# A decoder layer on one core: three small carry tiles padded, so that all pools that TensorE reads start at the same address modulo 64 bytes

## The chip, the cores and the metric

The kernel runs on 1 core of one Trainium2 chip. The metric is the device time of one execution in microseconds (us), as the median of several runs. The engines go by their short names in the profile: PE is TensorE's matmul, PEld its load of the stationary operand, DVE is VectorE, ACT is ScalarE, POOL is GpSimd and SP is SyncE, which issues the transfers (DMAs).

## What is computed

One layer of a decoder over 1024 tokens of width 1024, in float32. The reference, cut to its outline:

```python
h = _rms_norm(x, norm_pre_mix)
mix = _hybrid_mixer(h, ...)        # RWKV-7 time mixing of 8 heads beside a causal
                                   # convolution of width 31; one projection in, one out
x = x + _rms_norm(mix, norm_post_mix)
h = _rms_norm(x, norm_pre_ffn)
hid = _causal_dwconv(h @ ffn_up, ffn_conv_w, ffn_conv_b)     # 1024 -> 2 * 2816, width 3
gate, up = hid[..., :2816], hid[..., 2816:]
f = (gelu(gate) * up) @ ffn_down                             # 2816 -> 1024
x = x + _rms_norm(f, norm_post_ffn)
```

Both convolutions reach back over earlier tokens, so whatever works through the tokens in two halves must carry the last columns of the first half over to the second.

## The kernel before

**Precision.** Every large matmul is split: each float32 operand becomes a high part (rounded to float32r by ACT) and a low part (the rest, by DVE or POOL), and a product is three matmuls: high by high, high by low, low by high. `split` (L159) and `weight` (L164) do that. A weight tile is loaded into `wr`, and its halves `wh` and `wl` lie in the pool `wp`.

**Tokens and stages.** The tokens go in two halves of 512. `mixer` (L1245) interleaves the projections, the convolution, the recurrence and the output projection `w_out`, and, near its end, the first twelve tiles of the feed-forward's first half. Then `run` (L1201) opens the feed-forward pools with `setup_ffn` (L817) and goes on in this order:

- `ffn_pair` (L901) of the first half and `gates` (L939): matmuls of the activations `h0`, which lie in the pool `hp`, with weights in `wp`. Beside them the second half is normed; its activations `h1` (named `f` in the profile, as those of `h0` are) go to the pool `h1p`.
- `ffn_pair` of the second half for 12 of the 22 tiles, 48 matmuls each (two branches, 24 each), with `h1` in `h1p` and weights in `wp`. Beside it, `weight_sums` and `four_sums` (L1054) make sums of weight blocks on POOL.
- `shared` (L1004) for the other 10 tiles of both halves: five block products instead of six, 60 matmuls a tile. Its operands are S[2] (pool `rowp`), S[1] (`nrowp`), S[3] and S[4] (written back over `h0` in `hp`), and A22 (`h1[4:]` in `h1p`), all with weights in `wp`.
- `ffn_down` (L1103): seven block products instead of eight, each over 11 tiles of the inner dimension with 12 matmuls. The activations are split into pairs `a` in the pool `h1p`. The weights of the tiles 0, 2, 4, ... lie in `wp` (`wh`, `wl`), those of the tiles 1, 3, 5, ... in `h1p` (`w`), by this line:

```python
wh, wl = self.weight(wt(j), [P, 512], held=self.h1p if j % 2 else None) if j < n else held[j - n]
```

  In the last product the last five tiles' weights lie in `hp` (`held`). In `ffn_down` the activation is the stationary operand and the weight the moving one; in the other stages it is the other way round.

Each matmul instruction comes as a load of the stationary operand (128 columns) and the matmul proper, which streams the moving operand (mostly 512 columns). The load for the next matmul runs beside the matmul before it.

**Order.** The instructions are put in order when the program is built, by a planner with a timeline of its own; each engine then works through its queue in that order and waits on semaphores. Waits and buffers follow from the tiles that an instruction names.

**Memory.** Each pool is a stretch of on-chip memory with the same addresses in all 128 partitions. Pools are laid one behind the other in the order in which they are opened; each tile in a pool is rounded up to a multiple of 32 bytes a partition. `setup` opens `const` (at 16512), `small`, `wp` (at 24192), `hp` (38528) and `rowp` (71296 to 87680). `setup_mixer` opens `mconst` at 87680 and behind it `mix`, at 102752, which holds most of the mixer's tiles. When the mixer is done, the feed-forward takes the same stretch again: `fconst` at 87680, then `nrowp` at 92192, `actp` at 108576, `h1p` at 149536, `tp` at 182304 and `f2p` at 198688.

The three tiles of the change are small. `ccarry` in `mconst` keeps the last 30 columns of the convolution's input for four groups of channels; it is written and read by POOL in `glu_in` (L403, L394). `fcarry` in `fconst` keeps the last two columns of the feed-forward's tiles, written and read by ACT in `taps` (L892, L896). `fss` in `fconst` holds the sums of squares of the last norm: one column of it is written by each ACTIVATE of line L1150 and read by DVE at L1097.

Of the kernel before, what the change touches and what calls it, by code (L numbers as in the profile page):

```python
# [13 lines left out]
F32 = mybir.dt.float32  # L14
# [8 lines left out]
P = 128  # L23
# [13 lines left out]
CONV_W = 31  # L37
D_FF = 2816
FT = D_FF // P
# [59 lines left out]
class Trunk:  # L99
# [116 lines left out]
    def setup_mixer(self, ctx):  # L216
        nc, tc, a = self.nc, self.tc, self.a
        pool = lambda name, bufs=1: ctx.enter_context(tc.tile_pool(name=name, bufs=bufs))
        cp = pool("mconst")
        self.mix = pool("mix")  # L220
        self.banks = {"pb": 2, "pc": 1, "pe": 2}
        self.xs = [self.psum.tile([P, 512], F32, name=f"xs{g}") for g in range(2)]
        self.wa = cp.tile([P, HALF], F32, name="wa")

        self.dw = cp.tile([P, 16 + 1024], F32, name="dw")
        nc.gpsimd.memset(self.dw[0:64, 528:1040], 0.0)
        self.Y = self.psum.tile([P, 512], F32, name="Y")


        self.lora = cp.tile([G_LORA, D_RWKV], F32, name="lora")
        nc.sync.dma_start(self.lora, a["lora"][:G_LORA, 2])
        self.lw = cp.tile([96, 2, D_RWKV], F32R, name="lw")
        for e in range(2):
            raw = self.wp.tile([P, D_RWKV], F32, tag="wr", bufs=3, name=self.nm("wr"))
            nc.sync.dma_start(raw, a["lora"][:, e])
            nc.scalar.copy(self.lw[:, e], raw[0:96])
            low = self.lw[64:96, e]
            nc.gpsimd.tensor_tensor(low, raw[64:96], low.bitcast(F32), ALU.subtract)  # L240
        self.lx = cp.tile([96, 2, QUARTER], F32R, name="lx")
        n = POFF["k_k"]
        self.omu = cp.tile([P, n], F32, name="omu")
        nc.vector.tensor_scalar(self.omu, self.params[:, :n], -1.0, 1.0, ALU.mult, ALU.add)

        self.hw0 = cp.tile([P, 8], F32, name="hw0")
        nc.vector.tensor_scalar(self.hw0, self.params[:, POFF["w0"]:POFF["w0"] + 8], 0.5, None, ALU.mult)
        self.ka = cp.tile([P, 8], F32, name="ka")
        ka = self.params[:, POFF["k_a"]:POFF["k_a"] + 4]
        nc.vector.tensor_scalar(self.ka[:, 0:4], ka, 0.5, None, ALU.mult)  # L250
        nc.vector.tensor_scalar(self.ka[:, 4:8], ka, -0.5, 1.0, ALU.mult, ALU.add)
        cw = self.params[:, POFF["cw"]:POFF["cw"] + 4 * CONV_W]
        nc.vector.tensor_scalar(cw, cw, 0.5, None, ALU.mult)
        self.carry = cp.tile([P, n], F32, name="carry")
        self.ccarry = cp.tile([P, 4, CONV_W - 1], F32, name="ccarry")


    def channels(self, rows, gname, hs, toks, tags=("pn",), diags=None):
# [558 lines left out]
    def setup_ffn(self, ctx):  # L817
        nc, tc = self.nc, self.tc
        pool = lambda name, bufs=1: ctx.enter_context(tc.tile_pool(name=name, bufs=bufs))
        cp = pool("fconst")  # L820

        self.turn = cycle([lambda: self.xs[0], lambda: self.xs[1]]
                          + [lambda t=t: Trunk.bank(self, t) for t in ("pe", "pe", "pb", "pb")])
        self.bank = lambda tag="pb": self.Y if tag == "pn2" else Trunk.bank(self, "pc") if tag == "pn" else next(self.turn)()
        self.nrowp = pool("nrowp")

        self.ap = pool("actp", 2 * JOINT)
        self.h1p = pool("h1p", 2 * KT)
        self.tp = pool("tp", 8)
        self.f2p = pool("f2p", 6)  # L830
        self.post_ffn = cp.tile([P, D], F32, name="post_ffn")
        nc.sync.dma_start(self.post_ffn, self.a["post_ffn"].broadcast_to([P, D]))
        self.fcarry = cp.tile([P, 2, FT, 2], F32, name="fcarry")
        self.fss = cp.tile([P, 8, 2], F32, name="fss")

    def row(self, tag, n):
        return (self.rowp if tag == "row" else self.nrowp).tile([P, D], F32, tag=tag, bufs=n, name=self.nm(tag))
# [630 lines left out]
```

## Time and profile before

| | |
|---|---|
| median of three runs | 1280.13 us (1280.02 to 1281.09) |
| profiled execution | 1282.25 us, of which the span from first to last instruction is 1280.5 |
| mean granted TensorE clock | 0.988 |
| PE busy | 1231.8 us (96%), 8460 matmuls |
| POOL busy | 495.6 us (39%) |

How to read what is quoted further on: the page gives busy time and share of each engine; the 40 digits are the busy tenths of 40 equal slices of the span; the chain is the work that ended last, followed back from the last instruction. A line of the chain in order of time has its start, its length, the engine and line, and the number of instructions merged (x). A window line has for each engine its busy time and the number of instructions, then the granted clock, the busy share of the DMA engines and GB/s. A line of the timeline has the start, the length, the engine, the source line, the operation, the tiles (out<-in, with numbers left out) and sizes, and in brackets the idle time before it and what ended it. Matmuls overlap: one lasts about 0.39 us from its start to its end, while the next starts some 0.23 us after it. The time that matters for a row of matmuls is from start to start.

### The profile page before, as it was taken

The page shows a single profiled execution, that of the slowest core. Times are in us where ns is not written, and L with a number is a line of the kernel's source. Part 1 is how long each engine was busy: PE and PEld are TensorE (multiplying, and loading weights), DVE is VectorE, ACT ScalarE, POOL GpSimd, SP SyncE. Part 2 cuts the span into 40 slices and gives each one's busy share as a digit, 9 for nine tenths or more (in the row PEclk, how much of TensorE's full clock was granted, in tenths as well). Part 3 has the DMA queues.
Part 4 walks back from the last instruction along what each step waited for, and adds up shares of the span by engine and source line. Part 5 has one row for each costly group of instructions (what it writes and reads, how often), then busy time and mean ns, then how long its engine had stood idle before and what let it go on. Part 6 is the DMA issues. An engine that isn't in the chain of part 4 may idle for free.

```text
span 1280.5 us, 23025 instructions
## 1 busy us (share of the span) xinstructions
PE 1231.8 (96%) x8460; PEld 993.7 (78%) x8460; DVE 892.2 (70%) x1540; ACT 731.3 (57%) x1518; POOL 495.6 (39%) x438
## 2 busy tenths in 40 slices
PE   6989989999999989999999999999999999999997
PEld 5767767787778867788789878787778888888885
DVE  5286998997679989996621275655366678479568
ACT  6563564655844865656743277777455566444451
POOL 4343320011113332344455269897688860000001
PEclk9999999999999999999999999999999999999999
DMA  7544442343342461222345498887423245335523
GB/s 241 171 137 138 118 127 76 107 133 116 109 131 89 133 192 44 84 79 80 108 137 159 133 335 304 287 310 238 157 67 82 71 159 190 91 114 187 162 73 132
DMA packets 105505, 185.70 MB, mean 145 GB/s; under 512 B 15184, under 2 KB 21712, under 8 KB 105392
## 3 DMA queue, kind: packets, MB, share of 16 engines
q1 hardware_dynamic: 105392, 184.23, 45.5%
q8 instruction: 67, 1.10, 0.4%
q14 instruction: 46, 0.38, 0.1%
HBM read 141.58 MB, written 42.60 MB: 144 GB/s over the span
## 4 chain that ended last, share of the span: by engine, by line
PE 58%; DVE 8%; issue 2%; POOL 2%; DMA 2%; ACT 2%; SPq 0%; POOLq 0%; DVEq 0%; ACTq 0%
PE pb L135 27%; PE pe L135 13%; PE xs L135 12%; PE Y L135 2%; PE pc L135 2%; DVE pc L416 2%; DVE nrow L1116 1%; POOL wl L162 1%; DVE x L1100 1%; PE pc L150 1%; DMA pt<-mixd 1%; DMA m<-mixd 1%; POOL b L1056 1%; PE pe L150 0%; DVE m L162 0%
## 5 line engine op out<-in xcount | busy, mean ns | idle before, releaser
L162 POOL TENSOR_TENSOR wl<-wr,wh 128x512 fp32r<-128x512 f32 (+1 forms) x181 | 237.5, 1314 | 251.0 <-ACT wh L162 219.8
L162 ACT CAST wh<-wr 128x512 fp32r<-128x512 f32 (+1 forms) x220 | 135.4, 616 | 174.4 <-issue 46.1
L135 PE MATMUL pb<-h,wh 128*128 128x512 f32 (+3 forms) x720 | 228.8, 397 | 3.2 <-ACT wh L162 1.6
L135 PE MATMUL pb<-f,wh 128*128 128x512 f32 x696 | 221.9, 399 | 2.5 <-ACT wh L162 1.5
L416 DVE SCALAR_TENSOR_TENSOR pc<-c,params,pc 128x512 f32<-128x512 f32 x232 | 174.3, 751 | 8.7 <-ACT pc L413 4.7
L135 PEld LDWEIGHTS pb<-h,wh 128*128 128x128 f32 (+2 forms) x720 | 131.2, 188 | 36.0 <-ACT wh L162 3.7
L135 PEld LDWEIGHTS pb<-f,wh 128*128 128x128 f32 x696 | 130.9, 190 | 32.4 <-ACT wh L162 2.8
L135 PE MATMUL pb<-h,wl 128*128 128x512 f32 (+3 forms) x360 | 146.1, 406 | 2.1 <-POOL wl L162 2.0
L135 PE MATMUL pb<-f,wl 128*128 128x512 f32 x348 | 139.0, 400 | 0.9 <-POOL wl L162 0.9
L157 POOL TENSOR_TENSOR ss<-var,mhalf 128x1 f32<-128x1 f32 x16 | 11.0, 692 | 226.9 <-DVE ss L1097 202.8
L1056 POOL TENSOR_TENSOR b<-b,b 128x512 f32<-128x512 f32 x66 | 86.9, 1319 | 2.6 <-DMA b<-ffn_down 1.0
L135 PE MATMUL pe<-f,wh 128*128 128x512 f32 x272 | 85.4, 395 | 0.1
L135 PEld LDWEIGHTS pb<-h,wl 128*128 128x128 f32 (+2 forms) x360 | 67.3, 187 | 20.1 <-POOL wl L162 4.1
L135 PEld LDWEIGHTS pb<-f,wl 128*128 128x128 f32 x348 | 66.3, 190 | 16.7 <-POOL wl L162 2.0
L135 PE MATMUL xs<-f,wh 128*128 128x512 f32 x200 | 62.7, 395 | 0.4 <-DVE act L953 0.4
L135 PEld LDWEIGHTS pe<-f,wh 128*128 128x128 f32 x272 | 51.0, 188 | 11.7 <-ACT wh L162 0.3
L899 DVE SCALAR_TENSOR_TENSOR pt<-pb,params,pt 128x511 f32<-128x511 f32 (+1 forms) x48 | 35.7, 744 | 31.6 <-ACT ecarry L892 31.1
L162 POOL TENSOR_TENSOR wl<-b,wh 128x512 fp32r<-128x512 f32 x36 | 47.0, 1305 | 22.4 <-ACT wh L162 20.7
L135 PE MATMUL pe<-f,wl 128*128 128x512 f32 x136 | 53.8, 396 | 0.7 <-POOL wl L162 0.7
L706 POOL TENSOR_TENSOR XG<-r,GE 64x256 f32<-64x256 f32 x30 | 20.4, 683 | 87.1 <-DVE r L725 82.3
L178 ACT CAST wh<-wr 128x512 fp32r<-128x512 f32 (+2 forms) x44 | 26.5, 604 | 43.5 <-PE pb L135 31.2
L162 ACT CAST wh<-b 128x512 fp32r<-128x512 f32 x36 | 22.2, 617 | 47.4 <-PE pb L135 19.2
(428 smaller groups left out, 2896.8 us busy)
## 6 DMA issues: line engine op xcount, KB each, us to landing
wr<-ffn_up SPq DMA_DIRECT2D x117, 256.0 KB, 2.8
wr<-w_in SPq DMA_DIRECT2D x80, 256.0 KB, 3.0
b<-ffn_down SPq DMA_DIRECT2D x44, 256.0 KB, 4.4
sums<-b SPq DMA_DIRECT2D x44, 256.0 KB, 3.9
wr<-sums SPq DMA_DIRECT2D x44, 256.0 KB, 2.7
lows<-wl SPq DMA_DIRECT2D x40, 256.0 KB, 3.3
wl<-lows SPq DMA_DIRECT2D x40, 256.0 KB, 2.6
b<-ffn_up SPq DMA_DIRECT2D x40, 256.0 KB, 2.7
```

Of the source, the lines that this page charges most:

```text
L135: return self.nc.tensor.matmul(out, lhsT, rhs, start=start, stop=stop, skip_group_check=skip)
L150: self.nc.tensor.transpose(out, in_, self.con("ident")[:n, :n])
L157: self.nc.gpsimd.tensor_tensor(out, v[:, :n], self.mhalf[:, :n], ALU.pow)
L162: return self.nc.scalar.copy(hi, src), eng.tensor_tensor(lo, src, hi.bitcast(F32), ALU.subtract)
L178: self.nc.scalar.copy(hi, raw)
L416: nc.vector.scalar_tensor_tensor(out, c[:, j:j + HALF], w(j), acc, ALU.mult, ALU.add)
L706: nc.gpsimd.tensor_tensor(x[64:128], R[64:128, gs], w.GE[64:128, c, gs].unsqueeze(2).broadcast_to([64, 4, CH]), ALU.mult)
L899: nc.vector.scalar_tensor_tensor(acc[:, o:], ps[:, :HALF - o], w(j), acc[:, o:], ALU.mult, ALU.add)
L1056: sub = lambda o, x, y, op=ALU.subtract: self.nc.gpsimd.tensor_tensor(o, x, y, op)
L1100: nc.vector.scalar_tensor_tensor(x, f[c], s[:, 1:2], x, ALU.mult, ALU.add)
L1116: nc.vector.tensor_tensor(out, a, b, op)
```

## The change

Three tiles are allocated larger than what is used of them. `ccarry` gets 32 columns of which 30 are used, through a view; `fcarry` gets 32 rows instead of 22 in its third dimension; `fss` gets 48 columns, of which the first two are used. In bytes of a partition: 480 to 512, 352 to 512, 64 to 1536. No instruction is added or taken away.

```diff
-        self.ccarry = cp.tile([P, 4, CONV_W - 1], F32, name="ccarry")
+        self.ccarry = cp.tile([P, 4, 32], F32, name="ccarry")[:, :, :CONV_W - 1]
...
-        self.fcarry = cp.tile([P, 2, FT, 2], F32, name="fcarry")
-        self.fss = cp.tile([P, 8, 2], F32, name="fss")
+        self.fcarry = cp.tile([P, 2, 32, 2], F32, name="fcarry")
+        self.fss = cp.tile([P, 8, 48], F32, name="fss")
```

All pools that are opened after these tiles move: `mix` by 32 bytes, and `nrowp`, `actp`, `h1p`, `tp` and `f2p` by 1632. The pools `const`, `wp`, `hp` and `rowp` stay where they are.

## The prediction

> **What bounds the kernel now.** I read the page's first two parts, then the chain, then stretches by engine, then single instructions in order of time.
>
> ```profile
> span 1280.5 us, 23025 instructions
> PE 1231.8 (96%) x8460; PEld 993.7 (78%) x8460; DVE 892.2 (70%) x1540; ACT 731.3 (57%) x1518; POOL 495.6 (39%) x438
> ...
> PE   6989989999999989999999999999999999999997
> ...
> PEclk9999999999999999999999999999999999999999
> ...
> PE 58%; DVE 8%; issue 2%; POOL 2%; DMA 2%; ACT 2%; SPq 0%; POOLq 0%; DVEq 0%; ACTq 0%
> ```
>
> TensorE is busy in nine tenths of nearly every slice at full granted clock, and it holds 58% of the chain. But busy matmuls overlap, so the page cannot say whether the matmuls themselves could go faster. The windows of the feed-forward stages show where nothing else stands in the way:
>
> ```profile
> 780.00:850.00 70.00, 69.58 (x296) 55.09 (x296) 41.19 (x62) 51.33 (x108) 62.83 (x51) 1.00 0.86 297
> 850.00:925.00 75.00, 74.84 (x321) 60.02 (x320) 36.69 (x53) 46.18 (x97) 53.40 (x43) 1.00 0.68 229
> 925.00:1060.00 135.00, 133.61 (x573) 106.33 (x572) 89.59 (x129) 76.56 (x160) 104.10 (x80) 1.00 0.32 100
> 1060.00:1160.00 100.00, 100.00 (x432) 80.91 (x431) 71.03 (x114) 51.61 (x98) 0.00 (x0) 1.00 0.42 135
> ```
>
> The columns are PE, PEld, DVE, ACT, POOL, clock, DMA share, GB/s. PE has no idle worth naming from 780 to 1160, and its clock is 1.00. So the time here is the number of matmuls times the time from one start to the next, and this step is what the change can touch. Is the step the same everywhere? In the chain, pieces of PE follow each other without a gap, so their length over their count is the step:
>
> ```profile
> 762.95 0.44 PE pc L150 x4
> ...
> 772.90 5.47 PE pe L135 x24
> ...
> 841.64 11.24 PE pe L135 x48
> ...
> 864.11 11.25 PE pe L135 x48
> ```
>
> At 773 a 128x512 matmul takes 5.47/24 = 227.9 ns; at 842 and 864 it takes 11.24/48 = 234.2 ns. Same shape, same clock, same instruction line, no waits. What differs is where the operands lie: at 773 the activations come from `hp` (first half of the tokens), at 842 from `h1p` (second half); the weights come from `wp` both times.
>
> **The addresses.** This is the allocator's arithmetic for the kernel before: pools lie one behind the other and each tile is rounded up to 32 bytes a partition. `wp` starts at 24192, `hp` at 38528, `rowp` at 71296: all multiples of 64. `rowp` ends at 87680 = 1370·64. In the mixer the constants up to `ccarry` (rounded: 14400 + 64 + 32 + 32 + 64 + 480 = 15072) put `mix` at 102752 = 1605·64 + 32. In the feed-forward part `post_ffn`, `fcarry` and `fss` (4096 + 352 + 64) put `nrowp` at 92192 = 1440·64 + 32, and `actp`, `h1p`, `tp`, `f2p` behind it keep that 32, since all their tiles are multiples of 64. So a matmul from `hp` with `wp` has both operands in one class modulo 64, one from `h1p` with `wp` has them in two. The change makes `ccarry` 512, `fcarry` 512 and `fss` 1536 bytes: `mix` starts at 102784 = 1606·64, `nrowp` at 93824 = 1466·64. Two classes become one.
>
> Function `shared` gives a control inside one stage, with one weight pool; its order (S[3] and S[4] from `hp`, A22 from `h1p`, then of the next tile S[2] from `rowp`, S[1] from `nrowp`, twelve matmuls each) names each group. The starts:
>
> ```profile
> 950.85 0.62 PE L135 MATMUL pe<-f,wh 128*128 128x512 f32 x2
> ...
> 953.60 0.62 PE L135 MATMUL xs<-f,wh 128*128 128x512 f32 x2
> ...
> 956.32 0.63 PE L135 MATMUL pe<-f,wh 128*128 128x512 f32 x2
> ...
> 959.12 0.63 PE L135 MATMUL pe<-s,wh 128*128 128x512 f32 x2
> ...
> 961.94 0.63 PE L135 MATMUL pb<-s,wh 128*128 128x512 f32 x2
> ...
> 964.75 0.62 PE L135 MATMUL pb<-f,wh 128*128 128x512 f32 x2
> ```
>
> S[3]: 2.75 us over 12 is 229.2 ns; S[4]: 2.72, or 226.7; A22 (two classes): 2.80, or 233.3; S[1] (two classes): 2.81, or 234.2. S[2] (one class) has 2.82, but with a hole in it: its second start waits for a weight. In the last stage, `ffn_down`, both activations `a` and every second weight lie in `h1p`, the other weights (`wh`) in `wp`:
>
> ```profile
> 1148.66 0.62 PE L135 MATMUL pb<-wh,a 128*128 128x512 f32 x2
> ...
> 1151.46 1.55 PE L135 MATMUL pb<-w,a 128*128 128x512 f32 x6
> ...
> 1154.22 0.63 PE L135 MATMUL pb<-wh,a 128*128 128x512 f32 x2
> ...
> 1157.04 1.55 PE L135 MATMUL pb<-w,a 128*128 128x512 f32 x6
> ...
> 1159.80 0.63 PE L135 MATMUL pb<-wh,a 128*128 128x512 f32 x2
> ```
>
> `wh` groups (two classes): 2.80 and 2.82 us. `w` groups (both in `h1p`): 2.76 and 2.76, or 230.0 ns. So it is not `h1p` itself that is slow but the pairing; and a group of one class that follows one of two classes does not get down to 226.7.
>
> **The terms.** No instruction is added or removed; only addresses move.
>
> (1) Pairs of two classes. `ffn_pair` of the second half: 12 tiles x 48 = 576. `shared`: 10 x 12 for A22 and 10 x 12 for S[1] = 240. `ffn_down`: six products with 72 each, and in the last product 36 and the 60 of the held weights: 528. Together 1344. The last product's 96 are left out, for the end is not PE's there:
>
> ```profile
> 1238.47 0.69 DVE L162 TENSOR_TENSOR w<-wr,w 128x512 fp32r<-128x512 f32 x1 [1.48 <-ACT w L162]
> 1239.08 0.68 DVE L1116 TENSOR_TENSOR c<-c,pb 128x512 f32<-128x512 f32 x1
> ...
> 1271.62 0.68 DVE L1116 TENSOR_TENSOR nrow<-nrow,pe 128x512 f32<-128x512 f32 x1
> ...
> 1276.64 0.74 DVE L1100 SCALAR_TENSOR_TENSOR x<-nrow,ss,x 128x512 f32<-128x512 f32 x1
> ```
>
> From 1239 DVE runs through its own queue to the end, with waits on POOL only; it starts earlier when PE has been faster before, but gains nothing from a faster PE beside it. So 1248 matmuls go from 234.2 to between 227.9 (the row at 773) and 226.7 (S[4]): 6.3 to 7.5 ns, 7.9 to 9.4 us.
>
> (2) Groups of one class that are kept above the floor by their neighbours: 360 in `ffn_down` without the last product, from 230.0 to the same two ends: 0.8 to 1.2 us. In `shared`, S[2] and S[3], 240, from 229.2: 0.3 to 0.6 us.
>
> (3) Cost: `const` stays at 18016 = 281·64 + 32. The transposes read it together with `mix` and `nrowp` tiles, one class before and two after. The row at 762.95 is the transposes of one class, 110 ns each. How many there are comes from the groups of line 150 that read `const`, of which these are the first and the last of thirteen:
>
> ```profile
> L150 PE MATMUL pe<-const,l 32*32 32x32 f32 (+1 forms) x208 | 20.4, 241 | 12.2 <-ACT l L311 9.7 <-DVE mixr L760 2.1 <-DVE h L279 0.2
> ...
> L150 PE MATMUL pe<-const,co 128*128 128x128 f32 x3 | 1.1, 372 | 0.0
> ```
>
> In sum 448, of which 128 (in `merge`) are 32 wide, so 320 of this width. No row shows a transpose of two classes, so they are bounded by nothing below and by the 7 ns of a matmul four times as long above: 0 to 2.2 us. I take 0.5, nearer to nothing, as most lie in the mixer, where PE shares the chain with others. Mixer matmuls that pair `mix` with `mconst` come into one class, which I count at nothing.
>
> (4) Cover: POOL makes the low halves of the weights, between the sums of `four_sums`, in order. In 780 to 850 it is busy 62.8 of 70 us; PE 3% faster needs 67.9, still more than POOL's, but in places POOL is already late:
>
> ```profile
> PEld xs L135 <- POOL wl L162: 2.4, 6, 0.6
> ```
>
> Six waits, 2.4 us in all from 780 to the end of PE's work. At most this takes back the whole gain of 780 to 925 (617 matmuls x 7 ns = 4.3 us), at least nothing; I take 0.5, since POOL's busy time stays below PE's. ACT (51 of 70), DVE (71 of 100) and DMA (0.86) are further off. The ACT and DVE ops on shifted tiles I count at nothing: they work on both classes now, hidden under PE.
>
> Sum: 9.0 to 11.2, middle 10.1, less 0.5 and 0.5: 9.1 us. The profiled execution took 1282.25 (span 1280.5 and 1.75 around it), which gives 1273.15; it stands 2.1 above the median of the runs, 1280.13, and that gives 1271.0.
>
> **A rule against it.** The rows above have the step depend on the pairing of the two operands. The Trainium skill, "TensorE: Matmul & The Clock Gate", section "Part 2: What happens when you issue a matmul", says that TensorE has two independent read ports into SBUF, and that loading the next weights takes no bandwidth from the running matmul. By that rule where the two operands lie to each other cannot matter. The trace does not agree: 226.7 against 233.3 ns within 6 us of the same stage. By the rule the sum is nothing and the time stays at 1280.1; by the rows it is 9.1 us.
>
> **Rivals.**
> (a) The two reads don't meet, and 234 ns comes from something else in those groups (the bank written, the neighbours' traffic). Against it: four pools in the same order as their classes. For it: classes and pools are never crossed otherwise in one pool. Then the time stays at 1280.1, or 1280.6 with the cost of (3).
> (b) Half the effect: the step stops at the 230.0 of the `w` groups, because something else than the neighbours holds them there. 1248 x 4.2 = 5.2, less 0.5: 1275.4.
> (c) POOL becomes the bound from 780 to 925: of the 10.1, 4.3 are lost, less the 0.5 of (3): 1274.8.
> (d) Slower: feed-forward tiles lie over the mixer's and may be written only when those are free.
>
> ```profile
> 730.37 1.29 DVE L953 COPY act<-xs 128x512 f32<-128x512 f32 x2 [0.89 <-DMA mixd<-t]
> ```
>
> The first write of `act` waited 0.89 us for a store of a mixer tile. All these pools move up by 1632 bytes and cover other mixer tiles; a slot that now waits for a later store holds up the whole second half, microsecond for microsecond. It decides from 9.1 + 2.6 = 11.7 us on, more than ten such waits; 0.89 us once gives 1271.9. Against it: all of them lie inside `mix` as before, whose last store is this one.
>
> **How the numbers follow.** Within 0.2% (2.6 us) is about what a measurement of this kernel tells from no change. Forecast 0.70 (own range 1268.3 to 1274, from 11.8 us, a little over the full sum, down to 6), (b) 0.10, (c) 0.10, (a) 0.06, (d) 0.04. Faster by over 0.2%: 0.70 + 0.10 + 0.10 = 0.90; same 0.06; slower 0.04. The range takes in (b) and (c) with a microsecond of late waits: 1268.3 to 1276.5.
>
> **What would show it.** Right: in the stretch of the second half's `ffn_pair` the chain has 48 matmuls in 10.9 us and not 11.24; `wh` and `w` groups in `ffn_down` both take 2.72 to 2.74 us; the stage from 730 to the end is 8 to 10 us shorter, the mixer within 1 us. Wrong in (1): groups at 2.80 as before. Wrong in (2): `w` groups still at 2.76. Wrong in (4): PE waits for POOL's `wl` for several us between 780 and 925. The prediction fails too if the order of instructions is another one after the change.

## The result and the profile after

The kernel after takes 1273.43 us (median of six runs, 1268.18 to 1275.69); the kernel before took 1281.63 on the same chip (1280.02 to 1286.07). The ratio is 0.993, with a 95% interval of 0.9905 to 0.9955: the medians are 8.2 us apart, and the interval is 5.8 to 12.2 us. The profiled execution after took 1273.13 us. On every engine the same instructions stand in the same order as before, so what differs is addresses and what follows from them.

The page of the kernel after, its first two parts and the first line of its chain:

```profile
span 1271.4 us, 23025 instructions
PE 1220.3 (96%) x8460; PEld 990.1 (78%) x8460; DVE 891.2 (70%) x1540; ACT 731.1 (58%) x1518; POOL 495.4 (39%) x438
...
PE 55%; DVE 8%; DMA 3%; POOL 3%; issue 2%; ACT 2%; SPq 0%; POOLq 0%; DVEq 0%; ACTq 0%
```

PE's busy time fell by 11.5 us with the same 8460 matmuls, and PE's share of the chain fell from 58% to 55%; POOL and DMA took a point each. Busy time counts overlapping matmuls once, so it is the starts that say how fast PE went. Two of the stretches, kernel after (columns as in the prediction):

```profile
780.00:850.00 70.00, 68.67 (x297) 54.82 (x296) 41.06 (x61) 51.77 (x109) 62.97 (x50) 1.00 0.88 297
...
1060.00:1160.00 100.00, 100.00 (x443) 82.83 (x442) 72.61 (x117) 53.33 (x99) 0.00 (x0) 1.00 0.41 126
```

In the 100 us from 1060, where POOL does nothing, PE now starts 443 matmuls instead of 432, or 2.5% more. In the 70 us from 780, where POOL is busy for 63, it starts 297 instead of 296: there nearly nothing of the gain arrived. The clock is 1.00 in both, as before. The chain of the kernel after, pieces from 798 on:

```profile
798.76 2.47 PE pb L135 x11
...
802.27 1.00 PE pb L135 x4
...
807.11 1.30 POOL b L1056
...
808.50 1.30 POOL b L1056
809.80 1.25 POOL wl L162
...
813.39 4.88 DMA b<-ffn_down
...
820.50 1.30 POOL wl L162
...
821.82 2.52 DMA wr<-ffn_up
...
824.37 1.29 POOL wl L162
...
825.71 8.00 PE pb L135 x34
...
839.39 11.18 PE pe L135 x48
...
889.43 10.88 PE pe L135 x48
```

From 889 on, 48 matmuls take 10.88 us, 226.7 ns each, where before they took 11.24. But from 803 to 826 the chain leaves PE for POOL's sums (`b`, L1056), its low halves (`wl`), the transfers behind them and short pieces of ACT and SP that are not shown. Single instructions of POOL and PE there, on the timeline of the kernel after:

```profile
820.50 1.29 POOL L162 TENSOR_TENSOR wl<-wr,wh 128x512 fp32r<-128x512 f32 x1
821.76 2.66 POOL L1056 TENSOR_TENSOR b<-b,b 128x512 f32<-128x512 f32 x2
824.37 1.28 POOL L162 TENSOR_TENSOR wl<-wr,wh 128x512 fp32r<-128x512 f32 x1
...
825.71 0.50 PE L135 MATMUL pb<-f,wl 128*128 128x512 f32 x1 [0.68 <-POOL wl L162]
```

POOL works without a gap here, its `wl` of 824.37 stands behind two sums, and PE waits 0.68 us for it. In `shared` and `ffn_down` the groups that were slow are not slow any more:

```profile
952.43 0.62 PE L135 MATMUL pe<-f,wh 128*128 128x512 f32 x2
...
955.15 0.61 PE L135 MATMUL pe<-s,wh 128*128 128x512 f32 x2
...
958.22 0.61 PE L135 MATMUL pb<-s,wh 128*128 128x512 f32 x2
...
960.94 0.62 PE L135 MATMUL pb<-f,wh 128*128 128x512 f32 x2
...
1141.69 0.62 PE L135 MATMUL pb<-wh,a 128*128 128x512 f32 x2
...
1144.41 1.52 PE L135 MATMUL pb<-w,a 128*128 128x512 f32 x6
...
1147.13 0.62 PE L135 MATMUL pb<-wh,a 128*128 128x512 f32 x2
```

A22 (from 952.43) and S[1] (from 958.22) take 2.72 us instead of 2.80 and 2.81; `wh` and `w` groups both take 2.72 instead of 2.80 and 2.76.

What became of the gain is read from the starts of the matmuls on both timelines, stage by stage. A step of over 250 ns is a hole, and its excess over 227 is what it costs. The other steps give the mean step.

| from the first matmul of a stage to that of the next | before: us, holes (us), mean step | after |
|---|---|---|
| second half's `ffn_pair`, 576 matmuls | 136.39, 8 (1.6), 234.2 ns | 134.52, 20 (3.6), 227.4 ns |
| `shared`, 600 | 141.66, 19 (3.3), 230.7 | 140.90, 25 (4.3), 227.6 |
| `ffn_down`, 923 | 214.51, 0, 232.4 | 209.46, 2 (0.2), 226.7 |

The steps gained 3.9, 1.8 and, in `ffn_down` without the last product, 4.5 us: 10.2. The holes took back 2.0 in `ffn_pair` and 1.0 in `shared`; the two holes of `ffn_down` stand in its last product. That leaves 7.1 to 7.2 for the feed-forward, which the marks of one transpose group and of the last stage confirm. The rows of `Y<-const,nrow` give line, operation, count, the shortest, median and longest in ns, the first and last start, and shapes; first that of the kernel before, then that of after:

```profile
L150 PE MATMUL Y<-const,nrow x16: 270/272/273, 746.2 to 778.5; 128*128 128x128 f32 x16
```

```profile
L150 PE MATMUL Y<-const,nrow x16: 270/272/273, 744.2 to 776.5; 128*128 128x128 f32 x16
```

DVE's timeline in the last product, kernel after:

```profile
1229.36 0.69 DVE L162 TENSOR_TENSOR w<-wr,w 128x512 fp32r<-128x512 f32 x1 [1.42 <-ACT w L162]
...
1267.52 0.75 DVE L1100 SCALAR_TENSOR_TENSOR x<-nrow,ss,x 128x512 f32<-128x512 f32 x1
```

From 778.5 to DVE's split at 1238.47 it was 460.0 us, from 776.5 to 1229.36 it is 452.9: 7.1 less. From there to the last product's end DVE takes 38.2 in both. The span is 9.1 shorter because this execution also came to the first `Y` transpose 2.0 us earlier. Of these, 1.6 arise between the matmuls that start at 633 and 669 in the kernel before, and there the two executions were granted a different clock. The stretch from 633 to 682, first of the kernel before, then of after:

```profile
633.00:682.00 49.00, 48.55 (x254) 42.08 (x255) 15.71 (x22) 21.95 (x44) 27.51 (x22) 0.97 0.45 131
```

```profile
633.00:682.00 49.00, 48.95 (x270) 42.92 (x271) 15.99 (x21) 23.27 (x48) 28.69 (x22) 1.00 0.48 141
```

The clock is 0.97 in one and 1.00 in the other; 3% of 49 us is 1.5 us, an estimate. So most of the early start is the clock's and not the addresses' work; kernels below show the same scatter.

### The profile page after: what moved, and what is told of

Its sections match the earlier page's. It is cut to its first block, busy times and chain, and to the rows that moved or that the text cites. A ratio compares the mean times of both kernels' runs of the same rounds, so it can differ in the third digit from the quotient of the medians.

```text
span 1271.4 us, 23025 instructions
## 1 busy us (share of the span) xinstructions
PE 1220.3 (96%) x8460; PEld 990.1 (78%) x8460; DVE 891.2 (70%) x1540; ACT 731.1 (58%) x1518; POOL 495.4 (39%) x438
## 4 chain that ended last, share of the span: by engine, by line
PE 55%; DVE 8%; DMA 3%; POOL 3%; issue 2%; ACT 2%; SPq 0%; POOLq 0%; DVEq 0%; ACTq 0%
PE pb L135 26%; PE pe L135 13%; PE xs L135 11%; PE Y L135 2%; DVE pc L416 2%; PE pc L135 2%; POOL wl L162 1%; DVE nrow L1116 1%; DVE x L1100 1%; POOL b L1056 1%; PE pc L150 1%; DMA pt<-mixd 1%; DMA m<-mixd 1%; PE pe L150 0%; DMA b<-ffn_down 0%
## 5 line engine op out<-in xcount | busy, mean ns | idle before, releaser
L135 PE MATMUL pb<-f,wh 128*128 128x512 f32 x696 | 219.0, 395 | 2.6 <-ACT wh L162 1.5
L1056 POOL TENSOR_TENSOR b<-b,b 128x512 f32<-128x512 f32 x66 | 86.8, 1317 | 2.8 <-issue 0.9
```

The costliest lines, as they stand in the source:

```text
L135: return self.nc.tensor.matmul(out, lhsT, rhs, start=start, stop=stop, skip_group_check=skip)
L1056: sub = lambda o, x, y, op=ALU.subtract: self.nc.gpsimd.tensor_tensor(o, x, y, op)
```

## Experiments: which part, and which distance

Each ratio is to the kernel before, run beside the others on the same chip; its median is between 1279.62 and 1281.55 us from group to group.

**Only the mixer's tile.** Padding `ccarry` alone moves `mix` by 32 bytes, and the feed-forward stays as it was.

```diff
-        self.ccarry = cp.tile([P, 4, CONV_W - 1], F32, name="ccarry")
+        self.ccarry = cp.tile([P, 4, 32], F32, name="ccarry")[:, :, :CONV_W - 1]
```

> Only ccarry is padded: mix starts at a multiple of 64, the feed-forward pools stay at 32 beyond one. Theory (the step from one matmul to the next depends on whether the running moving operand and the next stationary operand lie in one class modulo 64): no gain, as the mixer's wide matmuls read hp with wp and mix with mix, one class before and after; 1279 to 1283 us, the second half's ffn_pair still at 234 ns a step, wh groups of ffn_down at 2.80 to 2.82 us. Rival (part of the gain comes from the mixer, where the two traces differ by 2.4 us at its end): 1279 or less, with the feed-forward part starting 2 us earlier in each comparison.

Measured: ratio 0.9994 (0.9975 to 1.0014), 1281.4 us against 1281.55. Its chain in the second half's `ffn_pair`:

```profile
839.40 11.25 PE pe L135 x48
...
890.24 11.25 PE pe L135 x48
```

The steps are those of before, and no gain is seen within 0.2%. The gain comes from the feed-forward's pools.

**Equal modulo 64, not modulo 256.** On the kernel before, `fss` grows by 32 bytes alone, so that `nrowp`, `actp`, `h1p` and the rest move by 32. They are then multiples of 64, as `wp` is, which is what the change aims at.

```diff
-        self.fss = cp.tile([P, 8, 2], F32, name="fss")
+        self.fss = cp.tile([P, 8, 3], F32, name="fss")
```

> Only fss is padded, by 32 bytes: nrowp starts at 92224, a multiple of 64 that lies 64 beyond a multiple of 128, while wp and hp start at multiples of 128. Theory (classes modulo 64): the whole gain, 1271 to 1275 us, steps of 226.7 ns in ffn_down. Rival (the modulus is larger, 128 or more; in the change as made all feed-forward pools and wp are equal modulo 2048): no gain or a part of it, groups of 2.80 us in ffn_down, 1278 to 1282 us.

Measured: ratio 1.0005 (0.9994 to 1.0017), 1282.69 us. Its chain:

```profile
891.58 11.20 PE pe L135 x48
```

That is 233.3 ns a step, 0.9 below before and 6.6 above after. So the condition as the change and the prediction name it, equal modulo 64, does not bring the fast step. (In `ffn_down` the mean step fell from 232.4 to 230.4 ns, a small part of the way.) The distance from `wp` to `nrowp`, which `h1p` shares modulo 256, was 92192 - 24192 = 68000 = 265·256 + 160 before; it is 265·256 + 192 here, and 69632 = 272·256 in the kernel after.

**All pools 32 bytes off.** On the kernel after, a small constant grows by 32 bytes, and every pool behind it, `wp` and `hp` too, moves by 32.

```diff
-        self.mhalf = cp.tile([P, 8], F32, name="mhalf")
+        self.mhalf = cp.tile([P, 16], F32, name="mhalf")[:, :8]
```

> The change and 32 more bytes in const, so that wp, hp, rowp, mix and all feed-forward pools start 32 beyond a multiple of 64: all in one class, none at a multiple of 64. Theory (only the pairing counts): as after the change, 1271 to 1275 us, 226.7 ns in ffn_down. Rival (what counts is that an operand starts at a multiple of 64, so that a 512 byte read touches 8 lines of 64 bytes and not 9): all matmuls are slow, 234 ns also in the first half's ffn_pair and in the mixer's projections, 1285 us or more.

Measured: ratio 0.9924 (0.9906 to 0.9943), 1272.22 us, the same as the kernel after. Its chain:

```profile
886.74 10.88 PE pe L135 x48
```

Neither operand starts at a multiple of 64 here, and the step is 226.7 ns. For this shift of 32 bytes, what counts is the distance between the two operands and not the address of either.

**Sixteen bytes.** On the kernel after, the split tiles in `h1p` begin 16 bytes into their buffers and are 2112 bytes apart, so that against `wp` they lie at 16, 80, 144 and 208 modulo 256, and against each other at 0, 64, 128 and 192.

```diff
+        if pool is getattr(self, "h1p", None):
+            return tuple(pool.tile([P, HALF + 16], F32R, tag="h", name=self.nm(what))[:, 4:4 + HALF] for _ in range(2))
```

> After the change, but each activation and weight of h1p is read 16 bytes into its tile: h1p lies 16 beyond wp and hp modulo 64, pairs within h1p and pairs with nrowp stay in one class. Theory as put (one class modulo 64 or two): two classes, 234 ns a step in the second half's ffn_pair and 2.80 us in the wh groups, 1278 to 1282 us. Rival (only the 32 byte bit counts): as after, 226.7 ns, 1271 to 1275 us. Between: the price grows with the offset, about 230 ns.

Measured: ratio 0.9974 (0.9959 to 0.9989), 1278.72 us. Its chain:

```profile
860.10 11.22 PE pe L135 x48
...
876.90 11.16 PE xs L135 x48
```

Steps of 233.8 and 232.5 ns: these offsets cost nearly what 160 did. The four distances 16, 80, 144 and 208 alternate within each row of matmuls here, and in the second half's `ffn_pair` the steps average 232.3 to 232.7 ns at each of them. As a slow step also slows those behind it, these means are blurred: no distance beside 0 comes out fast, but none of the four was tried alone. (The kernel stays 0.26% faster than before, with `nrowp` in place.) This kernel also answers a rival: that the gain comes from the moved tiles that DVE, ACT and POOL work on. `actp` and `nrowp` lie as in the kernel after, `tp` and `f2p` 1024 bytes further; by their distance only `h1p` is changed, and its steps are slow again.

**512, 256 and 128 bytes.** Three more sizes of `fss` alone, on the kernel before: 5, 13 and 9 columns for 2. They put `nrowp`, `actp`, `h1p` and the rest at a whole multiple of 512 from `wp`, at 256 beside one, and at 128 beside one of 256.

```diff
-        self.fss = cp.tile([P, 8, 2], F32, name="fss")
+        self.fss = cp.tile([P, 8, 5], F32, name="fss")     # the second: 13, the third: 9
```

> Only fss is padded, to five columns: nrowp and the pools behind it lie 68096 bytes = 133 x 512 beyond wp, ccarry and fcarry stay as before. All three theories (the operands must be equal modulo 128, modulo 256, or modulo 512, which is the length of one stationary block) expect the whole gain: 226.7 ns a step in ffn_down, 1271 to 1275 us. Rival (equal modulo 2048 is needed, as the change has it): groups above 2.76 us, 1277 to 1282 us.

> As before with fss padded to thirteen columns: the feed-forward pools lie 256 beyond wp modulo 512. Modulo 128 or 256: the whole gain, 226.7 ns a step, 1271 to 1275 us. Modulo 512: slow, 230 to 234 ns, 1278 to 1283 us.

> As before with fss padded to nine columns: the feed-forward pools lie 128 beyond wp modulo 256 and modulo 512. Modulo 128: the whole gain, 226.7 ns a step, 1271 to 1275 us. Modulo 256 or 512: slow, 230 to 234 ns, 1278 to 1283 us.

The chains, in the order 512, 256, 128:

```profile
888.52 10.88 PE pe L135 x48
```

```profile
891.58 10.88 PE pe L135 x48
```

```profile
892.33 11.20 PE pe L135 x48
```

| distance of `h1p` from `wp` | step in the chain | ratio to before (95%) |
|---|---|---|
| 0 modulo 512 | 226.7 ns | 0.9952 (0.9935 to 0.9968) |
| 256 modulo 512 | 226.7 | 0.9949 (0.9932 to 0.9966) |
| 128 modulo 256 | 233.3 | 0.9993 (0.9977 to 1.0009) |

The medians are 1274.49, 1273.95 and 1279.05 us against 1279.62. So the period is 256 bytes: the pairing is fast where both operands have the same address modulo 256, and slow at the other distances tried alone, 128, 160 and 192. The first two rows are the change in one line, 96 or 352 bytes; their ratios overlap with that of the full change.

**How a slow pairing reaches its neighbours.** The steps of the `w` groups in `ffn_down`, whose own operands lie 0 apart, averaged by their place among the twelve of a group, six products together: in the kernel before 233, 236, 225, 231, 236, 229, 233, 231 and then 227 four times, in the kernel after 226 to 227 throughout. So the 230.0 is a mean of two things: the slowness of the group ahead lasts some eight steps longer and then ends. With `h1p` at 128 beside a multiple of 256, three steps of such a group are slow (231 to 232 ns), and the rest take 227.

## Experiments: where the rest of the gain went

**How steady the holes are.** Each kernel has one trace. Nine of those above have PE's and POOL's instructions in the same order, so their holes can be compared:

| holes, us | five kernels with steps of about 230 ns and more | four with steps of about 227 ns (0 modulo 256) |
|---|---|---|
| second half's `ffn_pair` | 1.3 to 5.1, mean 2.5 | 3.6 to 6.8, mean 4.7 |
| `shared` | 3.3 to 6.0, mean 4.0 | 4.3 to 5.2, mean 4.7 |

The means differ by 2.2 and 0.7 us, near the 2.0 and 1.0 found between before and after, but single executions scatter by more than that. The experiments that follow are to be read with this scatter in mind.

**Short sums, before and after.** The sums of `weight_sums` on POOL cover 16 of 512 columns, once on the kernel before and once on the kernel after. Their number, their transfers, the low halves and the sums in `shared` stay; but the planner now puts the four short sums of a step one behind the other on POOL, with the low halves behind them, so the order of POOL's queue is changed with the time. It is the same in both new kernels.

```diff
-            self.four_sums(*b, b[3])
+            self.four_sums(*(t[:, :16] for t in b), b[3][:, :16])
```

> The kernel before, but the sums of weight blocks that weight_sums makes on POOL cover 16 columns of 512; all loads and stores of the blocks stay, and so do the sums in shared. The output is therefore another one. To be read against few_after. Theory (POOL's sums make its low halves late): the 576 matmuls of the second half's ffn_pair take about 135 us, 1.4 less than before, with holes of under 0.5 us in sum. Rival (transfers make them late): 136.4 as before, holes of 1.5 us.

> The same cut of the sums on the changed kernel; the order of instructions is that of few_before. Theory: with POOL's load gone, the 576 matmuls take about 131 us, 3.5 to 4 us less than in few_before (the change alone gave 1.9), holes under 0.7 us; shared stays near 140.9. Rival (transfers): the holes of the changed kernel (3.6 us over 20) stay, and the gain over few_before stays near 1.9.

Measured: 0.9988 (0.9973 to 1.0004) and 0.9907 (0.989 to 0.9923) of the kernel before; medians 1279.21 and 1269.17. With short sums the addresses are worth 10.0 us, and 8.2 in the full kernel; the short sums by themselves, on the addresses of before, are within the noise. The chain, with short sums on the addresses of before, then of after:

```profile
836.40 11.25 PE pe L135 x48
858.89 11.24 PE pe L135 x48
```

```profile
834.47 10.88 PE pe L135 x48
856.23 10.88 PE pe L135 x48
```

The second half's `ffn_pair` went from 135.01 us (1 hole) to 131.01 (3 holes, 0.4 us): the addresses gain 4.0 there, 4.3 by the steps less 0.3 by holes, where the full kernel kept 1.9. Holes of 0.1 and 0.4 us lie outside the scatter of the nine kernels. The transfers are the same ones, so it is POOL's queue, the time of the sums and the order that goes with it, and not the transfers by themselves, that made the holes. In `shared`, whose own sums were left as they are, 25 holes with 4.6 us stayed.

The same `Y` rows of the two kernels, short sums on the addresses of before, then of after, and behind them the last instruction of each on DVE's timeline:

```profile
L150 PE MATMUL Y<-const,nrow x16: 270/272/273, 741.9 to 774.3; 128*128 128x128 f32 x16
```

```profile
L150 PE MATMUL Y<-const,nrow x16: 270/272/273, 741.6 to 774.0; 128*128 128x128 f32 x16
```

```profile
1271.39 0.74 DVE L1100 SCALAR_TENSOR_TENSOR x<-nrow,ss,x 128x512 f32<-128x512 f32 x1
```

```profile
1261.94 0.74 DVE L1100 SCALAR_TENSOR_TENSOR x<-nrow,ss,x 128x512 f32<-128x512 f32 x1
```

From the last `Y` transpose to the last instruction shown: 497.1 and 487.9, a gain of 9.2, against 7.1 in the full kernels. The first pair of marks also shows the scatter at the start: up to its first `Y` transpose the kernel with short sums has PE's order and all the addresses of before, and it came there at 741.9, not 746.2. Over all traces that mark lies at 741.9 to 746.2 us without the padded `ccarry` and at 740.6 to 747.1 with it. The 2.0 us by which the kernel after was early lie inside that.

**Some low halves on DVE.** On the kernel after, every fourth low half of the second half's `ffn_pair` and the one of `b22` in `shared` go from POOL to DVE (`spare` is a cycle of three False and one True in that stage).

```diff
-                self.low = self.split(hi, lo, raw, self.low_pool)[1]
+                on_pool = self.low_pool and not next(self.spare)
+                low = self.split(hi, lo, raw, on_pool)[1]
+                if on_pool or not self.low_pool:
+                    self.low = low
...
-                    self.low = self.split(hi, lo, raw, True)[1]
+                    self.low = self.split(hi, lo, raw, raw is not b22r)[1]
```

> After the change, and in the second half's ffn_pair every fourth low half, in shared one of five, is made by DVE and not by POOL. Theory (POOL's late low halves take back 2 to 3 us of the gain between 800 and 1060): the waits of PE's weight loads for POOL fall from 10.5 us to under 5, the stretch from the first matmul of the second half's ffn_pair to the first of ffn_down gets 1.5 to 3 us shorter than after, 1270 to 1272 us. Rival (the waits are set by transfers and by the order of the queues): they stay or go to DVE, no gain on after, 1272 to 1275 us.

Measured: slower than before the change, 1.0058 (1.0036 to 1.008), 1286.65 us. In the profiled execution, the slowest of five (1290.31 us), the second half's `ffn_pair` took 145.3 us with 34 holes (14.4 us). Its waits from 740 to 1060 (us in all, how many, the longest; code lines are later by one to four here):

```profile
POOL b L1060 <- DMA b<-ffn_down: 13.7, 5, 3.5
...
PEld pe L136 <- POOL wl L163: 7.1, 9, 1.8
```

The planner reordered the stage: with fewer low halves on POOL it put sums earlier, they now wait for their weights to arrive, and the low halves stand behind them in the same queue. The expectation failed: with work taken from POOL, PE's weight loads waited 18.6 us for POOL in all, where it was 10.5 in the kernel after.

**`b22` alone.** The last line of the same edit by itself.

> After the change, with one of the five low halves of each tile of shared (that of b22) made by DVE instead of POOL. Theory: POOL's load in shared falls by a tenth, holes there from 4.3 to about 2.5 us, the stage from 140.9 to about 139; 1271 to 1273 us. Rival (the holes come from the wait of POOL for ACT's high half): no change in shared, within 0.5 us.

Measured: 0.9967 (0.9955 to 0.998), 1278.09 us. `shared` took 142.6 us with 25 holes (5.9 us), not less than the 140.9 of after. Within `shared` the other instructions of PE and POOL kept their order (PE's differs from 1058 us on, in `ffn_down`), so a lighter POOL did not help there, and the expectation failed.

Where the holes of `shared` stand can be read from the traces. In eight of the ten tiles, in the kernel after and here, the third matmul of the tile, the first that needs a low half of a weight, waits; the excess of these steps and of those right behind them is 1.6 us before, 2.2 in the kernel after and 3.4 here. One of these waits, kernel after:

```profile
955.82 0.19 PEld L135 LDWEIGHTS pe<-s,wl 128*128 128x128 f32 x1 [0.48 <-POOL wl L162]
```

Its low half was made from 954.46 on. ACT had written the high half by 953.07, but POOL was at two sums first, from 951.85 on. So a low half that stands behind sums is the likely cause there, too, whatever POOL's load is on the mean; no experiment has taken the sums of `shared` away, so it is not shown.

**One of four sums on DVE.** In `weight_sums`, the second of the four sums goes to DVE.

```diff
-        sub(b21, b21, b11)
+        self.nc.vector.tensor_tensor(b21, b21, b11, ALU.subtract)
```

> After the change, with one of the four sums of each step of weight_sums made by DVE. Theory: POOL's load beside ffn_pair falls by about an eighth, the 576 matmuls take 132 to 133.5 us instead of 134.5; 1271 to 1273 us. Rival (a sum across two engines makes POOL wait for DVE in its own queue, and the low halves behind it are later still): 136 us or more there, 1275 us or more.

Measured: 0.9943 (0.9925 to 0.9961), 1273.57 us, which is the kernel after within the intervals. The stage took 135.2 us with 15 holes (4.4 us). Of its waits:

```profile
POOL wl L162 <- DMA b<-ffn_down: 3.4, 3, 1.4
...
POOL b L1056 <- DVE f L162: 1.8, 1, 1.8
```

The holes did not get fewer in time, and POOL waits longer for transfers and now for DVE, too; that these ate what POOL was spared is likely but not shown. None of the three kernels that take work from POOL beats the change.

## Why the prediction was right, and where not

- **That addresses set the step**: right, and shown by four kernels that differ from before in one tile's size alone. The rule weighed against it (the Trainium skill, "TensorE: Matmul & The Clock Gate", "Part 2: What happens when you issue a matmul", two independent read ports) would have the step not depend on the distance; the runs disagree, 226.7 ns at a distance of 0 modulo 256 against 233.3 at 128 and at 192, and rival (a) falls with it.
- **Classes modulo 64**: wrong. It is modulo 256. The control inside `shared` could not tell the two: `hp` and `rowp` lay at 0 from `wp` modulo 256, `nrowp` and `h1p` at 160, so 64, 128 and 256 all fitted, and the prediction weighed 64 alone. `ffn_down`'s `w` groups, 0 apart, could not either. The change works because its 1632 bytes bring 160 to 0 modulo 256, which being equal modulo 64 does not ask for.
- **Terms (1) and (2)**: right in size: 10.2 us measured, 10.1 in the middle of the sum. The `w` groups fell from 2.76 to 2.72 us although their own addresses to each other did not move, so it was their neighbours that held them up; rival (b), which has them stay, is excluded. That such a group "does not get down to 226.7" is not so: its last four steps were at 227 before the change already.
- **Term (3), transposes**: nothing, where 0.5 was taken. Transposes of `nrowp` against `const` last 272 ns (median), and within a group they start 107 to 110 ns apart, before and after. The prediction's row of "one class" was in truth 192 apart modulo 256, and it is 32 apart after the change. Neither is 0, so the term rested on a wrong class, and whether a distance of 0 would make transposes faster was not tried.
- **Term (4), POOL's cover**: the step that was mis-sized. It said 0.5 of at most 4.3; the holes took 2.0 in `ffn_pair` and 1.0 in `shared`, 3.0 in all between these two traces. PEld's waits for POOL from 740 to 1060 rose from 6.7 us in 16 to 10.5 in 24; the three largest groups of the kernel after (us in all, how many, the longest):

```profile
PEld pe L135 <- POOL wl L162: 4.2, 11, 1.1
PEld xs L135 <- POOL wl L162: 4.1, 9, 0.8
PEld pb L135 <- POOL wl L162: 2.2, 4, 1.1
```

  The argument compared busy time, 62.8 against 67.9 us of 70, and a mean says little of single low halves that stand behind two sums of 1.3 us each. It also counted too few waits: its "six waits, 2.4 us in all" are those of the tile `xs` alone, and with `pe` (1.3 in 5) and `pb` (1.2 in 3) the same view of before has 4.9 us in 14. The prediction's own sign of being wrong here came: from 780 to 925 these waits were 1.6 us before and 4.5 after. The short sums show the cause for `ffn_pair`; for `shared` the cause of the other 1.0 us is only argued. Rival (c) was half true.
- **The tail**: right. DVE takes 38.2 us from its split in the last product to its end in both kernels, and what PE gains beside it is lost.
- **Rival (d)**, a late start through overlapping tiles: not seen; the order is the same, and the feed-forward came no later.
- **The sum**: 9.1 predicted, 7.1 found between the marks of two traces and 8.2 between the medians (5.8 to 12.2 by the interval). Two signs of being right did not come: from the first write of `act` (730.37 before, 728.30 after) to the end it is 7.1 us less and not 8 to 10, and the mixer differs by 2 us and not by under 1, mostly for the clock. That the profiled execution met the predicted 1273.15 to 0.02 us is luck: the 2.0 us of an early start made up for most of the 2.5 that the holes took beyond term (4).

## What to carry to other kernels

Where matmuls follow each other without a gap, compare start to start between groups of the same shape: a few nanoseconds between groups with operands in different pools can be a matter of addresses, and padding one small tile ahead of the pools settles it. Choose the padding by the distance between the stationary and the moving operand modulo 256 bytes here, and test the period with two or three sizes rather than take the smallest that fits the rows. Before counting a gain of an engine that is the bound, look at the next one's queue, instruction by instruction, not at its busy share.

## What was not expected of the hardware

- A float32r matmul of 128x512 starts 226.7 ns after the one before it where its operands' pools lie at the same address modulo 256 bytes, and 233.3 to 234.2 ns after it at distances of 128, 160 and 192 (in the second half's `ffn_pair`). Distances of 256 and 512 are as good as 0; 16, 80, 144 and 208, tried together, cost nearly as much (232.5 and 233.8); and a shift of all pools by 32 bytes changes nothing (226.7).
- A slow pairing slows the steps behind it: groups of `ffn_down` with operands in one pool had steps of 225 to 236 ns for the first eight, 227 for the last four, and 226 to 227 throughout when the slow groups were gone. A hole does something like it: in the kernel after, in the piece of 48 at 839, two steps of 362 and 338 ns are followed by 235, 229, 232 and 231, and then by 227 again. (Of the 0.30 us by which that piece is longer than the one at 889, 0.25 are the two steps themselves.)

What stays open is which two reads meet, the running matmul's moving operand with its own stationary operand or with the next one's load, and why the period is 256 bytes.
